# Finer first tiles, a deeper attention pipeline, two plain gate-value pairs and an early down projection in a two-block transformer kernel

## The chip, the cores and the metric

The kernel runs on one core of a Trainium2 chip. The metric is the time of one execution on the device in microseconds (us). Runs of the kernel before took 2423.92, 2426.95 and 2432.35 us; the median is 2426.95 us.

## The reference

Two transformer blocks work on one sequence of 1024 tokens with 1024 features, all in float32. What matters here is the first block and its feed-forward part:

```python
h = rms_norm(x, mix_norm_g)
proj = h @ w_in                       # stick-breaking attention, RWKV, spatial gating, ...
...
up = causal_dwconv(h2 @ w_up, conv_w) # D_FF = 2816: 2816 gate and 2816 value columns
gate, val = jnp.split(up, 2, axis=-1)
x = x1 + (jax.nn.silu(gate) * val) @ w_down
```

The stick-breaking attention (four heads of 64 features) and the spatial gating (a layer norm over 256 features, then a causal 128x128 mix of tokens) are two of four branches between the first projection and the feed-forward part. A second block with other mixers follows.

## The kernel before, in words

**Precision.** Every large matrix product is made of three float32 products. A matrix is split into a rounded part (a cast on ScalarE, ACT; `split`, L99 to L101) and the rest (a subtraction on VectorE, DVE, L101), and hi x hi, hi x lo and lo x hi are added up in PSUM. So each operand of TensorE (PE) costs one cast on ACT and one subtraction on DVE. One matmul instruction has a 128x128 weight tile and 512 moving columns.

**Order of the work.** Python code issues the instructions; a scheduler may move them on their engine unless they are pinned (`keep_in_program_order`) or urgent (`high_priority`). Each engine runs its list in order. `mingle` and `braid` (L130 to L144) interleave two generators: so many steps of the sparse one per step of the dense one.

**Start.** `Norm` (L170) loads the gain row as a 128x1024 broadcast `grow` on ACT's DMA queue. Eight tiles of 128 tokens (`xt`) are normalized (`put`), transposed on PE and split into `hh` and `hl` (`turn`). After four tiles `first_steps` multiplies the first half of the tokens (512) with the first two column tiles of the attention's q and k; the other four tiles are braided into that, and the second half follows. These 96 matmuls of 512 columns are recorded under L123.

**Phase 1.** The projection of the branches (dense, L123) is braided with the stick-breaking attention at the rate `RSB`. Per head and half of the queries, `score` computes the score tiles (L383) and the attention weights (a scan on DVE, L411, then POOL). `pv_steps` (L325) transposes them (L350) into the one PSUM bank `pt`, splits that into `pth` and `ptl`, and multiplies both with the values (L334, L335) one step later (`lag=1`). The spatial gating's norm runs on DVE beside it (L491 to L498).

**Up projection.** 22 units, each with 128 gate and 128 value columns. A unit uses a Strassen-like scheme of seven block products (p1 to p7) of 12 matmuls in place of eight (L1171). It needs sums of the activations' quadrants R2 (the split tiles T1 to T4 and B22), made once at its start (L1277 to L1287; two of these subtractions on GpSimd, POOL), and sums of the weights per unit (POOL). Unit 0 is computed plainly, with eight products, while the T tiles are made. `gate` (L1245) is a 3-tap convolution (ACT, then two steps on DVE), a tanh on ACT and one DVE step (L1249); `value` (L1251) a convolution with weights halved in `vw` and a multiplication on POOL (L1253). The product goes to one DRAM tensor `gg` on the queue of SyncE (SP).

**Down projection.** It loops over two token halves j, two column halves c and the 22 row tiles fi. For each fi it loads a tile of `w_down` (`wr`, L1428) and, for j = 0, one of `gg` (`s`, L1425), splits both, and issues 12 matmuls (L1439 to L1441). The tile pool `slots` for `s` opens after the up projection's pools are closed.

Of the kernel before, what the change touches and what calls it, by code (L numbers as in the profile page):

```python
# [31 lines left out]
RSB, RRW = 0.6, 1.27  # L32
# [33 lines left out]
def kernel(ctx: ExitStack, tc: tile.TileContext, A: dict, out: bass.AP, stop=None):  # L66
# [31 lines left out]
    G.memset(zero1, 0.0)  # L98
    def split(hi, lo, src, eng=None):  # L99
        S.copy(hi, src)  # L100
        (eng or V).tensor_tensor(lo, src, f(hi), op=ALU.subtract)  # L101
# [68 lines left out]
    class Norm:  # L170


        def __init__(self, pool, psum, gain, hi, lo):
            self.pool, self.psum, self.hi, self.lo = pool, psum, hi, lo
            self.g = pool.tile([128, D], F32, name="grow", bufs=1)
            S.dma_start(self.g, gain.partition_broadcast(128))
# [63 lines left out]
    with tc.tile_pool(name="n0", bufs=2) as n0, tc.tile_pool(name="n0p", bufs=2, space=PSUM) as n0p:  # L240
        nm = Norm(n0, n0p, A["mix_norm_g"], hh, hl)
# [10 lines left out]
        def first_steps(j):  # L252
            for c in range(2):
                if j == 0:
                    first.append((mmp.tile([128, T], F32, name="mm"), *sb_qk_weights(c)))
                yield from mm3_steps(*first[c], hh, hl, NK, js=(j,))

        for _ in norm_steps(range(4)):
            pass
        S.dma_start(pv, A["pvec"])  # L260
        S.dma_start(rv, A["rvec"].partition_broadcast(128))
        braid(first_steps(0), norm_steps(range(4, 8)), 0.5)
        for _ in first_steps(1):
            pass
# [128 lines left out]
    def sb_head(h, j, parts):  # L393
# [51 lines left out]
    mx = pj.tile([128, NT, 256], F32, name="mx")  # L445
    wc = pj.tile([128, 4, 128], F32, name="wc")
    S.dma_start(wc, A["sg_wT"].rearrange("g s t -> s g t"))
# [74 lines left out]
    def phase1_steps():  # L522
# [9 lines left out]
        yield from sg_mix()  # L532
        for p in range(2):
            yield from sg_out(p)
# [580 lines left out]
    gg_d = dram.tile([NF * 128, T], F32, name="gg")  # L1115
# [6 lines left out]
    class Unit:  # L1122
# [51 lines left out]
        def bank(self):  # L1174
            return upp.tile([128, 512], F32, name="ac", bufs=4)
# [6 lines left out]

        def plain(self, n):
# [61 lines left out]
        def gate(self):  # L1245
            a = self.conv(self.g, [PV("ffn_conv_w", 2 * NF * i + self.fi) for i in range(3)])
            self.th = up2.tile([128, T], F32, name="th")
            S.activation(self.th, a, AF.Tanh, scale=0.5)
            V.scalar_tensor_tensor(self.th, self.th, 1.0, a, op0=ALU.add, op1=ALU.mult)  # L1249

        def value(self):  # L1251
            b = self.conv(self.v, [vw[:, NF * i + self.fi:NF * i + self.fi + 1] for i in range(3)])
            G.tensor_tensor(b, self.th, b, op=ALU.mult)  # L1253
            (nc.sync if self.fi < NF - 1 else G).dma_start(gg_d[self.fi * 128:(self.fi + 1) * 128, :], b)
# [27 lines left out]
    v.w1()  # L1282
    G.tensor_tensor(R2[1, 0], R2[1, 0], R2[1, 1], op=ALU.subtract)
    v.sums()
    split(*T3, R2[0, 1])
    v.w2()
    split(*T4, R2[1, 0])  # L1287
    str_.close()
    up2 = stu.enter_context(tc.tile_pool(name="up2", bufs=1, reuse_waits="tile"))
    u.copies()  # L1290
    vw = up2.tile([128, 3 * NF], F32, name="vw")
    tc.keep_in_program_order(V.tensor_scalar(vw.rearrange("p (i f) -> p i f", i=3),
                                             PV("ffn_conv_w", 0, 6 * NF).rearrange("p (i e f) -> p i e f", i=3, e=2)[:, :, 1, :],
                                             0.5, None, op0=ALU.mult))
    tables = None
    for n in range(1, NF):
        u, v, w = us[n], us[n + 1] if n < NF - 1 else None, us[n - 1]
        u.p1()
        if n == 1:
            u.w4()  # L1300
        if v:
            v.load()
        if n > 1:
            w.p4()
            w.value()
            u.w3()
# [13 lines left out]
        if n > 1:  # L1320
            u.p2()
            u.c11()
        else:
            u.w3()
# [15 lines left out]
    stw.close()  # L1340
    slots = st3.enter_context(tc.tile_pool(name="slots", bufs=NF, reuse_waits="tile"))
# [70 lines left out]
    with tc.tile_pool(name="dw", bufs=1, side="right", reuse_waits="tile") as dw:  # L1412
# [5 lines left out]
        for j in range(2):  # L1418
            for c in range(2):
                acc = [bank(n) for n in (("ip", "ip", "tp", "tp"), ("lt", "lt", "ho", "iq"),  # L1420
                                         ("ip", "ip", "lt", "lt"), ("ho", "iq", "ip", "ip"))[2 * j + c]]
                for fi in range(NF):
                    if j == 0:
                        g_ = f(slot(c))
                        nc.sync.dma_start(g_, gg_d[fi * 128:(fi + 1) * 128, c * 512:(c + 1) * 512])  # L1425
                        gg.setdefault(fi, {})[c] = g_
                    raw = dw.tile([128, 512], F32, name="wr", bufs=3)
                    nc.sync.dma_start(raw, A["w_down"][fi * 128:(fi + 1) * 128, c * 512:(c + 1) * 512])  # L1428
                    wh, wl, gh, gl = [dw.tile([128, 512], F32R, name=name, bufs=2) for name in ("dwh", "dwl", "gh", "gl")]
                    with tc.high_priority():  # L1430
                        split(wh, wl, raw)
                        split(gh, gl, gg[fi][j])
                    if (j, c, fi) == (0, 0, 1):
                        dn = std.enter_context(tc.tile_pool(name="dn", bufs=1, reuse_waits="tile"))
                    if j and c:
# [8 lines left out]
                if nm is None:  # L1444
                    nm = Norm(dn, ipx, A["norm_gain_2"], hh, hl)
                    fg = dn.tile([128, D], F32, name="fg")
                    S.dma_start(fg, A["final_norm_g"].partition_broadcast(128))
                if c == 0:
                    xs = []
                    for i in range(4):  # L1450
                        x2 = dn.tile([128, D], F32, name="x2", bufs=4)
                        nc.sync.dma_start(x2, x1_d[(4 * j + i) * 128:(4 * j + i + 1) * 128, :])
                        xs.append(x2)
# [554 lines left out]
```

## Time and profile before

| what | before |
|---|---|
| median of the runs | 2426.95 us |
| the profiled execution, its own time | 2424.3 us |
| its span, first to last instruction | 2422.6 us |
| PE busy | 2322.5 us (96%) |
| DVE busy | 1467.4 us (61%) |
| ACT busy | 1067.3 us (44%) |
| POOL busy | 583.3 us (24%) |
| mean granted TensorE clock | 0.989 |

Times in the views are counted from the start of the span. The time that a run reports exceeds the span by 1.7 us. PE is busy for all but 100.1 us of the span, and a stretch counts as busy whether PE runs at its full clock or at the lower level; the granted clock is shown beside it. A matmul's own duration is longer than the distance to the next start, since matmuls are pipelined.

### The profile page before, as it was taken

Reading aid. Unit: us, or ns where it says so; the run is one execution under the profiler, and the core shown is the slowest. Engines: PE = TensorE matmul, PEld = TensorE weight load, DVE = VectorE, ACT = ScalarE, POOL = GpSimd, SP = SyncE. Lnnn points to the kernel's source line nnn. Section 1 sums busy time; section 2 is a strip of 40 time slices with the busy share of each in tenths; the row PEclk is TensorE's granted clock in tenths of the full one; section 3 lists DMA queues with packets and bytes.
Section 4 is the critical chain, followed back from the end, with each engine's and each line's share of the span. In section 5 each row is a group of like instructions: output and inputs, shape, how many; then the busy total and the mean of one; then the engine's idle time right before and its main releaser. Section 6 shows DMA issues by size and latency. Waiting matters only on the chain.

```text
span 2422.6 us, 31192 instructions
## 1 busy us (share of the span) xinstructions
PE 2322.5 (96%) x11330; PEld 1883.0 (78%) x11330; DVE 1467.4 (61%) x2357; ACT 1067.3 (44%) x1973; POOL 583.3 (24%) x582
## 2 busy tenths in 40 slices
PE   6999899999999999998999997999999999999999
PEld 5887676778777887877788886888798777787787
DVE  4245753578455534579888885556756525678842
ACT  4344433222443323444444342446556525669840
POOL 0122310113223111036555552000023100126510
PEclk9999999999999999999999998999999999999999
DMA  4332115454333258412222224734523647766433
GB/s 153 96 100 83 45 60 165 156 170 138 104 95 105 94 163 240 153 36 79 88 87 81 87 79 152 238 101 150 166 87 109 172 140 206 196 174 186 120 115 134
DMA packets 280442, 309.08 MB, mean 128 GB/s; under 512 B 14928, under 2 KB 209120, under 8 KB 280288
## 3 DMA queue, kind: packets, MB, share of 16 engines
q1 hardware_dynamic: 241296, 266.26, 36.2%
q10 hardware_dynamic: 38848, 40.31, 5.2%
q8 instruction: 89, 1.46, 0.3%
q14 instruction: 65, 0.53, 0.1%
q0 software_dynamic: 144, 0.52, 0.1%
HBM read 217.80 MB, written 89.23 MB: 127 GB/s over the span
## 4 chain that ended last, share of the span: by engine, by line
PE 45%; DMA 5%; DVE 4%; ACT 3%; issue 2%; POOL 1%; SPq 0%; POOLq 0%; ACTq 0%; DVEq 0%
PE ac L1171 11%; PE ip L1171 4%; PE ip L1493 3%; PE tp L350 1%; PE ip L1382 1%; PE ip L1383 1%; PE ip L1384 1%; PE iq L334 1%; PE lt L1777 1%; PE iq L335 1%; DMA wr<-in_w_in_dram 1%; PE ip L1441 1%; PE ip L1043 1%; PE ip L1439 1%; PE ip L1440 1%
## 5 line engine op out<-in xcount | busy, mean ns | idle before, releaser
L123 PE MATMUL mm<-hh,whi 128*128 128x512 f32 x896 | 304.6, 411 | 1.6 <-ACT hh L100 0.9
L123 PE MATMUL mm<-hl,whi 128*128 128x512 f32 x896 | 290.1, 395 | 0.0
L123 PE MATMUL mm<-hh,wlo 128*128 128x512 f32 x896 | 288.4, 393 | 1.3 <-DVE wlo L115 1.3
L100 ACT CAST whi<-wraw 128x1024 fp32r<-128x1024 f32 (+1 forms) x117 | 99.8, 853 | 262.7 <-PE mm L123 197.7
L123 PEld LDWEIGHTS mm<-hh,wlo 128*128 128x128 f32 x896 | 168.6, 189 | 38.8 <-DVE wlo L115 1.9
L123 PEld LDWEIGHTS mm<-hl,whi 128*128 128x128 f32 x896 | 168.1, 189 | 36.0 <-DVE hl L101 0.4
L101 DVE TENSOR_TENSOR wlo<-wraw,whi 128x1024 fp32r<-128x1024 f32 (+1 forms) x117 | 118.2, 1013 | 120.4 <-ACT whi L100 114.6
L123 PEld LDWEIGHTS mm<-hh,whi 128*128 128x128 f32 x896 | 158.9, 190 | 37.7 <-issue 7.1
L167 POOL TENSOR_TENSOR rs<-rs,negh 128x1 f32<-128x1 f32 x32 | 19.5, 612 | 381.1 <-DVE rs L166 381.1
L101 DVE TENSOR_TENSOR gl<-s,gh 128x512 fp32r<-128x512 f32 x88 | 60.7, 690 | 80.3 <-ACT gh L100 77.9
L1781 ACT ACTIVATE p<-p,mn 128x640 f32<-128x640 f32 (+7 forms) x128 | 99.5, 778 | 12.4 <-DVE mn L1779 12.1
L926 POOL TENSOR_TENSOR acc<-acc,pacc 128x1024 f32<-128x1024 f32 x20 | 50.7, 2536 | 199.8 <-DVE acc L921 144.6
L100 ACT CAST uhi<-s 128x1024 fp32r<-128x1024 f32 x42 | 44.1, 1053 | 122.9 <-PE ip L1171 87.6
L101 DVE TENSOR_TENSOR ptl<-tp,pth 128x512 fp32r<-128x512 f32 (+3 forms) x144 | 78.0, 555 | 31.8 <-ACT pth L100 30.6
L100 ACT CAST gh<-s 128x512 fp32r<-128x512 f32 x88 | 54.6, 621 | 94.3 <-PE tp L1440 35.6
L101 DVE TENSOR_TENSOR ulo<-s,uhi 128x1024 fp32r<-128x1024 f32 x42 | 88.0, 2097 | 4.9 <-ACT uhi L100 4.9
L100 ACT CAST pth<-tp 128x512 fp32r<-128x512 f32 (+3 forms) x144 | 66.9, 477 | 43.4 <-PE tp L350 41.3
L1253 POOL TENSOR_TENSOR cv<-th,cv 128x1024 f32<-128x1024 f32 x22 | 53.6, 2434 | 128.6 <-issue 90.2
L334 PE MATMUL iq<-pth,v 128*128 128x512 f32 x192 | 71.7, 375 | 7.8 <-DVE t L1806 4.1
L350 PE MATMUL tp<-cv,p 128*128 128x128 f32 x432 | 71.8, 277 | 1.6 <-DVE ptl L101 1.4
L1808 POOL TENSOR_TENSOR zz<-zz,rdb 128x512 f32<-128x512 f32 x16 | 20.6, 1290 | 216.0 <-DMA qh<-aq 128.2
L1493 PE MATMUL ip<-h3h,zh 128*128 128x512 f32 x192 | 65.6, 409 | 3.7 <-DVE zt L1499 3.7
(591 smaller groups left out, 6437.1 us busy)
## 6 DMA issues: line engine op xcount, KB each, us to landing
wraw<-in_w_in_dram SPq DMA_DIRECT2D x60, 512.0 KB, 4.1
wraw<-in_w_up_dram SPq DMA_DIRECT2D x44, 512.0 KB, 3.9
wr<-in_w_down_dram SPq DMA_DIRECT2D x88, 256.0 KB, 2.9
merged<-acc SPq DMA_DIRECT2D x28, 512.0 KB, 2.9
s<-gg SPq DMA_DIRECT2D x44, 256.0 KB, 4.5
gg<-cv SPq DMA_DIRECT2D x21, 512.0 KB, 2.6
pacc<-merged SPq DMA_DIRECT2D x20, 512.0 KB, 4.1
x<-x ACTq DMA_DIRECT2D x16, 512.0 KB, 2.7
```

Source lines behind the costliest of these rows:

```text
L100: S.copy(hi, src)
L101: (eng or V).tensor_tensor(lo, src, f(hi), op=ALU.subtract)
L123: PE.matmul(ps[:, c0 + j * 512:c0 + (j + 1) * 512], w[:, k, :], x[j][:, k, :], start=(k == 0 and w is wh and x is xh), stop=(k == nkt - 1 ...
L334: PE.matmul(po[-1][:, w], vh[:, k, :], ph_[:, w], start=(k == 0), stop=False)
L335: PE.matmul(po[-1][:, w], vh[:, k, :], pl_[:, w], start=False, stop=(k == nk - 1))
L350: PE.transpose(pt[:, i * 128:(i + 1) * 128], P[p0 + i][:, k * 128:(k + 1) * 128], ident)
L926: G.tensor_tensor(ac, ac, pa, op=ALU.add)
L1043: PE.matmul(po, ml[:, k, :], W[c][k][0], start=False, stop=(k == NK - 1))
L1171: PE.matmul(acc, a[:, k, :], b[:, k, :], start=(start and k + n == 0), stop=(k == 3 and n == 2), skip_group_check=True)
L1253: G.tensor_tensor(b, self.th, b, op=ALU.mult)
L1493: PE.matmul(ps[j], w[:, k, :], x[j][:, n, :], start=(n == 0 and w is wh and x is hh), stop=(n == 7 and bool(last)))
L1781: S.activation(pr_[:, :L], pr_[:, :L], AF.Exp, scale=-1.0, bias=mn[:, c:c + 1], accum_out=self.den[:, i:i + 1])
```

## The change

1. **Start.** The gain row is loaded once (4 KB on SP's queue) and spread over the partitions by two matmuls with a single contraction row into PSUM (`spread`). The first two column tiles are done by quarters of the tokens: 192 matmuls with 256 columns. They begin after two token tiles and are braided with the others at 0.25. SP's list begins with the row, two `xt`, the two weight tiles, four `xt`, two weight tiles, two `xt`, then `pv` and `rv`, which were on ACT's queue before the second weight load.
2. **Phase 1.** `RSB` goes from 0.6 to 0.7. `pv_steps` gets a lag of two steps and three buffers for `pth` and `ptl`; the bank `pt` stays single. `mx` shares the tile `vt`, and the mixing steps are mingled into the first output step.
3. **Up projection.** Units 0 and 1 are both plain. Unit 1's split weights (`own`) lie in the memory of T3, its accumulators in the banks `tp` and `ip`. The two subtractions of 128x2048 on POOL go to DVE, the gate is one Silu activation on ACT, the multiplication in `value` goes from POOL to DVE, and `vw` is gone. `gg` is 22 DRAM tensors; the last two are written on POOL's queue.
4. **Down projection.** The rows fi = 0 and 1 of the first pass are loaded and split inside the last unit (`down0`). From fi = 2 the loads of `s` and `wr` alternate on SP. The loads of `grow`, `fg` and four `x2` come at fi = 11 of the c = 0 passes.

```diff
-RSB, RRW = 0.6, 1.27
+RSB, RRW = 0.7, 1.27
...
+            self.g = psum.tile([128, D], F32, name="g", bufs=1)
+            for q in range(2):
+                PE.matmul(self.g[:, q * 512:(q + 1) * 512], ones, row[:, q * 512:(q + 1) * 512], start=True, stop=True)
...
+            for ps, wh, wl in first:
+                for k in range(NK):
+                    for w, x, last in ((wh, hh, 0), (wh, hl, 0), (wl, hh, 1)):
+                        PE.matmul(ps[:, q * 256:(q + 1) * 256], w[:, k, :], x[q // 2][:, k, s],
...
-        for _ in norm_steps(range(4)):
+        for _ in norm_steps(range(2)):
             pass
...
+        for q in range(3):
+            braid(first_steps(q), norm_steps(range(2 * q + 2, 2 * q + 4)), 0.25)
...
-            t1 = f(sb.tile([128, 512], F32R, name="ptl", bufs=2))[0:64]
+            t1 = f(sb.tile([128, 512], F32R, name="ptl", bufs=3))[0:64]
...
-        return [lambda i=i: score(i) for i in range(4 * j, 4 * j + 4)], pv_steps(sb, sb_po, sb_pt, v2[:, :, h, :], P, [(j, 0, evict)], 2)
+        return [lambda i=i: score(i) for i in range(4 * j, 4 * j + 4)], pv_steps(sb, sb_po, sb_pt, v2[:, :, h, :], P, [(j, 0, evict)], 3, 2)
...
-            S.activation(self.th, a, AF.Tanh, scale=0.5)
-            V.scalar_tensor_tensor(self.th, self.th, 1.0, a, op0=ALU.add, op1=ALU.mult)
+            S.activation(self.th, a, AF.Silu)
...
-            G.tensor_tensor(b, self.th, b, op=ALU.mult)
+            V.tensor_tensor(b, self.th, b, op=ALU.mult)
...
+    v.own(*[x.rearrange("p a c -> p (a c)").rearrange("p (w k c) -> p w k c", w=2, k=NK) for x in T3])
+    v.plain(0)
+    v.plain(1)
     split(*B12, R2[0, 1])
     split(*B22, R2[1, 1])
-    u.plain(2)
-    u.plain(3)
+    for x in (u, v):
+        x.plain(2)
+        x.plain(3)
...
-    G.tensor_tensor(R2[0, 1], R2[1, 1], R2[0, 1], op=ALU.subtract)
+    V.tensor_tensor(R2[0, 1], R2[1, 1], R2[0, 1], op=ALU.subtract)
...
+            for fi in range(2):
+                raw = wpool.tile([128, 2, 512], F32, name="wraw")
+                nc.sync.dma_start(raw[:, 0], A["w_down"][fi * 128:(fi + 1) * 128, 0:512])
+                nc.sync.dma_start(raw[:, 1], gg_d[fi][:, 0:512])
...
+                    if c == 0 and fi == NF // 2:
...
+                            pin(nc.sync.dma_start)(x2, x1_d[(4 * j + i) * 128:(4 * j + i + 1) * 128, :])
```

**PE in phase 1**, near the end of one head's second half. `mm` is the projection; `pth` and `ptl` are the two parts of a transposed tile of weights, `pt` is the bank, `sg` the weights. The brackets name the engine whose work the instruction waits for. Before:

```order
L123 MATMUL mm<-hh_77,wlo 128x512
L334 MATMUL po<-pth,v_551 128x384 [waits Activation_49]
L335 MATMUL po<-ptl,v_551 128x384 [waits DVE_49]
L350 MATMUL pt<-cv,sg_922 128x128 [waits PE_49]
L350 MATMUL pt<-cv,sg_979 128x128
L123 MATMUL mm<-hh_76,whi 128x512
```

Now:

```order
L127 MATMUL mm<-hh_77,wlo 128x512
L357 MATMUL po<-pth,v_652 128x384 [waits Activation_49]
L358 MATMUL po<-ptl,v_652 128x384
L373 MATMUL pt<-cv,sg_1053 128x128 [waits DVE_49]
L127 MATMUL mm<-hh_76,whi 128x512
```

The wait for DVE has moved from the product with `ptl` to the next transpose, one row further on. In both lists it is for the tile that was transposed in the step before; the product with `ptl` now belongs to the step before that.

**DVE at the start of the up projection**, from the first subtraction on the quadrants `r` (R2). `t1l` to `t4l` and `b2l` are the low parts of the split activations, `wlo`, `a2l` and `ulo` those of weights. Before:

```order
L1277 TENSOR_TENSOR r_7411<-r_7412,r_7411 128x2048
L101 TENSOR_TENSOR t4l<-r_7412,t4h 128x2048
L101 TENSOR_TENSOR b2l<-r_7414,b2h 128x2048
L101 TENSOR_TENSOR t1l<-r_7411,t1h 128x2048
L1280 TENSOR_TENSOR r_7414<-r_7414,r_7411 128x2048
L101 TENSOR_TENSOR t3l<-r_7412,t3h 128x2048
L101 TENSOR_TENSOR t2l<-r_7414,t2h 128x2048
L101 TENSOR_TENSOR wlo<-wraw,whi 128x1024
L101 TENSOR_TENSOR t4l<-r_7413,t4h 128x2048
```

Now:

```order
L1313 TENSOR_TENSOR r_7511<-r_7512,r_7511 128x2048
L105 TENSOR_TENSOR t3l<-wraw,t3h 128x1024 x2
L105 TENSOR_TENSOR t4l<-r_7512,t4h 128x2048
L105 TENSOR_TENSOR b2l<-r_7514,b2h 128x2048
L105 TENSOR_TENSOR t1l<-r_7511,t1h 128x2048
L1315 TENSOR_TENSOR r_7512<-r_7514,r_7512 128x2048
L105 TENSOR_TENSOR ulo<-s_8548,uhi 128x1024
L1316 TENSOR_TENSOR r_7514<-r_7514,r_7511 128x2048
L1323 TENSOR_TENSOR r_7513<-r_7513,r_7514 128x2048
L105 TENSOR_TENSOR t2l<-r_7514,t2h 128x2048
L105 TENSOR_TENSOR wlo<-wraw,whi 128x1024 x2
L1328 TENSOR_TENSOR t3l<-r_7512,t3h 128x2048
```

Two splits of unit 1's weights (`t3l<-wraw`) and the two subtractions from POOL (L1315, L1323) have come in; the real T3 is split after all the rest.

**SP's queue around the start of the down projection.** `gg<-cv` are the last units' results, `wr` the rows of `w_down`, `s` those of `gg`; `x<-x` are the loads of `x2`. Before:

```order
L1254 DMA gg<-cv 128x1024 x3
L1428 DMA wr<-in_w_down_dram 128x512 x3
L1452 DMA x_11850<-x_7404 128x1024
L1452 DMA x_11852<-x_7404 128x1024
L1428 DMA wr<-in_w_down_dram 128x512
L1452 DMA x_11854<-x_7404 128x1024
L1428 DMA wr<-in_w_down_dram 128x512
L1452 DMA x_11856<-x_7404 128x1024
L1425 DMA s_11315<-gg 128x512
```

Now:

```order
L1285 DMA gg_8272<-cv 128x1024
L1363 DMA wraw<-in_w_down_dram 128x512
L1364 DMA wraw<-gg_8254 128x512
L1363 DMA wraw<-in_w_down_dram 128x512
L1364 DMA wraw<-gg_8255 128x512
L1285 DMA gg_8273<-cv 128x1024
L1473 DMA s_11439<-gg_8256 128x512
L1479 DMA wr<-in_w_down_dram 128x512
L1473 DMA s_11463<-gg_8257 128x512
```

The four `x2` loads have left this place, and the first rows of `gg` are loaded ahead of the write of unit 19's result.

## Rows read from the trace of the kernel before

**Rows 1.** The page, section 1: busy time, share of the span, instructions.

```profile
PE 2322.5 (96%) x11330; PEld 1883.0 (78%) x11330; DVE 1467.4 (61%) x2357; ACT 1067.3 (44%) x1973; POOL 583.3 (24%) x582
```

**Rows 2.** Waits of PE: waiter <- releaser: us in total, times, longest.

```profile
PE ip L1439 <- ACT gh L100: 13.8, 1, 13.8
PE tp L193 <- DVE xn L184: 13.0, 4, 9.4
PE po L335 <- DVE ptl L101: 11.4, 6, 6.3
```

**Rows 3.** Windows: length, busy (count) of PE, PEld, DVE, ACT, POOL; clock, DMA share, GB/s.

```profile
0.00:57.20 57.20, 36.21 (x161) 27.91 (x162) 26.50 (x48) 24.00 (x54) 5.63 (x18) 1.00 0.47 147
```

**Rows 4.** Timeline of the start: start, duration, instruction, [idle before <-releaser].

```profile
8.58 1.42 DVE L184 SCALAR_TENSOR_TENSOR xn<-xt,rs,grow 128x512 f32<-128x512 f32 x2 [1.88 <-DMA grow<-in_mix_norm_g_dram]
...
25.68 0.79 PE L123 MATMUL mm<-hh,whi 128*128 128x512 f32 x1 [0.68 <-ACT hh L100]
...
44.63 1.04 PE L193 MATMUL tp<-cv,xn 128*128 128x128 f32 x8
...
54.68 0.39 PE L123 MATMUL mm<-hl,whi 128*128 128x512 f32 x1
...
57.18 0.61 PE L123 MATMUL mm<-hh,whi 128*128 128x512 f32 x2
```

**Rows 5.** Timeline of PE late in the second block, around two matmuls of 256 columns.

```profile
2339.44 0.28 PE L334 MATMUL iq<-pth,v 128*128 128x256 f32 x1
2339.55 0.28 PE L335 MATMUL iq<-ptl,v 128*128 128x256 f32 x1
2339.68 0.40 PE L1877 MATMUL lt<-foh,mh 128*128 128x512 f32 x1
```

**Rows 6.** The page, section 5: weight loads of L123 (busy, mean ns | idle).

```profile
L123 PEld LDWEIGHTS mm<-hh,wlo 128*128 128x128 f32 x896 | 168.6, 189 | 38.8 <-DVE wlo L115 1.9
```

**Rows 7.** Timeline of phase 1: PE's longest wait and DVE before it.

```profile
278.88 2.28 DVE L411 TENSOR_TENSOR_SCAN ex<-kp,zero 128x1024 f32<-128x1024 f32 x1
281.08 0.40 DVE L101 TENSOR_TENSOR ptl<-pt,pth 128x256 fp32r<-128x256 f32 x1
...
281.53 0.58 PE L335 MATMUL po<-ptl,v 128*128 128x256 f32 x1 [6.26 <-DVE ptl L101]
```

**Rows 8.** Timeline of the up projection's start: DVE, POOL and PE.

```profile
1058.89 2.29 DVE L101 TENSOR_TENSOR b2l<-r,b2h 128x2048 fp32r<-128x2048 f32 x1
1059.06 6.58 POOL L1278 TENSOR_TENSOR r<-r,r 128x2048 f32<-128x2048 f32 x1 [8.47 <-DVE t4l L101]
1061.10 6.69 DVE L101 TENSOR_TENSOR t1l<-r,t1h 128x2048 fp32r<-128x2048 f32 x1
...
1079.04 0.80 PE L1171 MATMUL ac<-b0h,whi 128*128 128x512 f32 x1 [5.82 <-ACT cg L1195]
```

**Rows 9.** Windows: the up projection's start, then its steady loop.

```profile
1060.00:1140.00 80.00, 67.71 (x277) 53.68 (x276) 76.21 (x58) 36.13 (x42) 42.48 (x17) 0.94 0.23 67
...
1160.00:1480.00 320.00, 320.00 (x1400) 261.44 (x1399) 267.87 (x237) 130.69 (x148) 164.56 (x80) 1.00 0.24 77
```

**Rows 10.** Groups of instructions from 1160 to 1480 us: busy, mean ns of one.

```profile
L1253 POOL TENSOR_TENSOR cv<-th,cv 128x1024 f32<-128x1024 f32 x16 | 38.8, 2423 | 80.8 <-issue 80.8
...
L1249 DVE SCALAR_TENSOR_TENSOR th<-th,cv 128x1024 f32<-128x1024 f32 x17 | 20.8, 1225 | 9.1 <-ACT th L1248 9.1
```

**Rows 11.** Timeline where the down projection starts.

```profile
1492.12 0.40 PE L1171 MATMUL ac<-t4h,a2l 128*128 128x512 f32 x1
...
1498.42 1.27 DVE L1242 SCALAR_TENSOR_TENSOR cv<-cx,vw,cv 128x1022 f32<-128x1022 f32 x1
...
1499.38 9.38 SPq L1425 DMA_DIRECT2D s<-gg  x12
...
1506.34 0.79 PE L1439 MATMUL ip<-dwh,gh 128*128 128x512 f32 x1 [13.82 <-ACT gh L100]
```

**Rows 12.** Windows: the first matmuls of the down projection.

```profile
1506.00:1510.00 4.00, 3.66 (x9) 2.84 (x10) 1.36 (x2) 0.91 (x2) 0.00 (x0) 0.50 1.01 351
```

More of the change, by code (lines that the diff above doesn't have):

```diff
@@ L250, in norm_steps, with first_steps @@
                 yield
[L252 to L256, printed above, removed]
-        for _ in norm_steps(range(4)):
-            pass
[L260 to L263, printed above, removed]
+        def first_steps(q):
+            s = slice(q % 2 * 256, q % 2 * 256 + 256)
+            for ps, wh, wl in first:
+                for k in range(NK):
+                    for w, x, last in ((wh, hh, 0), (wh, hl, 0), (wl, hh, 1)):
+                        PE.matmul(ps[:, q * 256:(q + 1) * 256], w[:, k, :], x[q // 2][:, k, s],
+                                  start=(k == 0 and w is wh and x is hh), stop=(k == NK - 1 and bool(last)))
+                    yield
+        for _ in norm_steps(range(2)):
+            pass
+        first += [(mmp.tile([128, T], F32, name="mm"), *sb_qk_weights(c)) for c in range(2)]
+        for q in range(3):
+            braid(first_steps(q), norm_steps(range(2 * q + 2, 2 * q + 4)), 0.25)
+        tc.keep_in_program_order(nc.sync.dma_start(pv, A["pvec"]))
+        tc.keep_in_program_order(nc.sync.dma_start(rv, A["rvec"].partition_broadcast(128)))
+        for _ in first_steps(3):
             pass
@@ L531, in phase1_steps @@
             yield
-        yield from sg_mix()
-        for p in range(2):
-            yield from sg_out(p)
+        mix = sg_mix()
+        for n, _ in enumerate(sg_out(0)):
+            if n % 2 == 0:
+                next(mix, None)
+            yield
+        yield from sg_out(1)
         yield from short_conv(1)
@@ L1109, in block2_tables @@
         yield
-    gg_d = dram.tile([NF * 128, T], F32, name="gg")
+    gg_d = [dram.tile([128, T], F32, name=f"gg{fi}") for fi in range(NF)]
     stu = ExitStack()
@@ L1174, in bank @@
         def bank(self):
+            if self.fi == 1:
+                return ipx.tile([128, 512], F32, name="tp" if len(self.b) < 2 else "ip", bufs=2)
             return upp.tile([128, 512], F32, name="ac", bufs=4)
@@ L1181, in wv, with own @@
             (self.a21, self.a22) = zip(halves4(hi), halves4(lo))
+        def own(self, hi, lo):
+            for i in range(2):
+                split(hi[:, i], lo[:, i], self.raw[i])
+            (self.a11, self.a12), (self.a21, self.a22) = [zip(halves4(hi[:, i]), halves4(lo[:, i])) for i in range(2)]
         def plain(self, n):
@@ L1339 @@
     st2.close()
-    stw.close()
-    slots = st3.enter_context(tc.tile_pool(name="slots", bufs=NF, reuse_waits="tile"))
+    slots = None
     def slot(j, ncol=512):
@@ L1430 @@
[L1430 to L1433, printed above, removed]
-                        dn = std.enter_context(tc.tile_pool(name="dn", bufs=1, reuse_waits="tile"))
+                    early = j + c == 0 and fi < 2
+                    if (j, c, fi) == (0, 0, 2):
+                        stw.close()
+                        slots = st3.enter_context(tc.tile_pool(name="slots", bufs=NF, reuse_waits="tile"))
@@ new lines @@
+                    late = {10: [0], 12: [1]}.get(fi, []) if c == 0 else []
+                    for x in ([] if early else [fi]) + late if j == 0 else []:
+                        g_ = f(slot(c))
+                        tc.keep_in_program_order(nc.sync.dma_start(g_, gg_d[x][:, c * 512:(c + 1) * 512]))
+                        gg.setdefault(x, {})[c] = g_
+                    if early:
+                        wh, wl, gh, gl = down0[fi]
+                    else:
+                        raw = dw.tile([128, 512], F32, name="wr", bufs=3)
+                        ld = nc.sync.dma_start(raw, A["w_down"][fi * 128:(fi + 1) * 128, c * 512:(c + 1) * 512])
+                        if j == 0:
+                            tc.keep_in_program_order(ld)
+                        wh, wl, gh, gl = [dw.tile([128, 512], F32R, name=name, bufs=2) for name in ("dwh", "dwl", "gh", "gl")]
+                        with tc.high_priority():
+                            split(wh, wl, raw)
+                            split(gh, gl, gg[fi][j])
@@ L1443 @@
                         spread.pop(0)()
[L1444 to L1453, printed above, removed]
                 for i in range(4):
```

96 lines of the change are left out of this document (55 added, 41 removed).

## The prediction

> **What bounds the kernel now.** The first view is the page's list of busy times: PE works 2322.5 of the 2422.6 us of the span [rows 1]. So only about 100 us are idle, and a change that leaves the matmuls as they are can win no more than a part of these, and what runs at the lower clock behind them. PE's waits say where they lie [rows 2]: one of 13.8 us ahead of the down projection's first matmul, 13.0 us for the normalized rows of the start, 11.4 us in six waits for `ptl` in phase 1. The other engines' busy shares tell nothing here; each place is then read in its own stretch. In the first 57.2 us PE is busy for 36.2, so 21.0 are idle [rows 3]. From 1060 to 1140 us, the up projection's start, it is busy for 67.7 of 80 with a granted clock of 0.94, while DVE is busy for 76.2 [rows 9]; there DVE is the bound. From 1160 to 1480 us PE is busy for all 320 us and DVE for 267.9: there PE is the bound, and nothing that DVE or POOL save is worth anything.
>
> **The change part by part.** Prices are of the profiled execution: 2422.6 us of span and 1.7 around it, 2424.3. The runs' median is 2.7 above that. A measurement of this kernel tells about 0.3%, 7.3 us, from no change.
>
> *Start.* Now DVE's first row multiplication starts at 8.58 after 1.88 us of waiting for the broadcast gain, the first projection matmul at 25.68, and the first matmul of the next pair of columns at 57.18 [rows 4]. Four tiles thus take 25.68 - 8.58 = 17.1 us, 4.3 each. With the gain row loaded by 4 KB, the first tile can start about 1.9 us earlier, at 6.7, and after two tiles, at 15.3, the products can begin; I take 16, as the first weight tile's cast comes between. Two limits follow. By PE: 192 matmuls of 256 columns at 0.115 (starts of 2339.44, 2339.55 and 2339.68 [rows 5]) are 22.1 us, six remaining tiles' transposes at 1.04 for eight [rows 4] are 6.2, so 44.3. By the tiles: 6.7 + 8 x 4.3 = 41.1, then 48 matmuls, 5.5 us: 46.6. The later one holds. The work itself costs nothing more: 96 matmuls at 0.227 (11 starts from 54.68 to 57.18 [rows 4]) were 21.8. **Gain 57.2 - 46.6 = 10.6**, between 6 (the two weight splits, 2 x 1.2 us on DVE and about as much on ACT, stretch the tiles' pace) and 13 (PE sets the end). The two spreading matmuls, the memset and the moved loads of `pv` and `rv` lie beside the tiles' loads; their cover is that nobody reads them before the first set ends.
>
> *Phase 1.* The longest wait, 6.26 us, ends when DVE has done a scan of 2.28 and then a `ptl` of 0.40 [rows 7]. DVE has worked off its list in order and came late, so the data was ready and DVE was not. The change gives PE no more room here than it seems: with one bank `pt`, the next transposes cannot start before `ptl` of the tile in the bank is made, so the wait moves by one row, from the product to the transpose. What remains is a different mixing: more attention steps per projection step, and the norm of the spatial gating meets other work. I cannot follow that through. **I take 3 of the 11.4** [rows 2], with the bounds +11 (all waits gone) and -6 (one more like the longest).
>
> *Up projection, start.* From 1060 to 1140 PE loses 12.3 us idle, and at a granted clock of 0.94 another 0.06 x 80 = 4.8 us [rows 9]: 17.1. A step of 128x2048 takes DVE 2.29 us, but 6.69 while a subtraction of 6.58 runs on POOL beside it [rows 8]. Two subtractions run on POOL there, so by this pair DVE loses some 2 x 4.4 us. With both on DVE its chain up to the second T tile is eight steps of 2.29 and three of 1.2, 22.0 us, without such a pair. Over it lie sixteen plain products, 16 x 12 x 0.227 = 43.6 us of PE, so no step of this chain is waited for. What is late next is T3: its memory holds unit 1's weights until the last plain product, so T3's and T4's splits, two convolutions, the first value multiplication and unit 2's second pair of weights (2 x 2.29, 7 x 1.2 and three of 0.7, some 15 us with the first cast of T3 ahead, 2 us) stand on DVE between the last plain product and the product p7. PE has five products ahead of p7 that need none of this (one of them the next unit's first), 60 matmuls or 13.6 us, so it waits about 2 us there. Unit 1 costs 12 matmuls more, 2.7 us. **Gain 17.1 - 2.7 - 2 = 12.4**; at best 14.4, at worst 3 (POOL's sums of weights run beside and stretch DVE's steps as above, and p7 is late by 10 more).
>
> *Up projection, steady loop.* A DVE step of 1.225 goes (L1249) and a multiplication of the same 128x1024 comes, which I price the same; POOL loses 2.42 [rows 10]. A unit has 84 matmuls, 19.05 us, so 320 us are 16.8 units and DVE's slack is (320 - 267.9) / 16.8 = 3.1 us a unit [rows 9]. Net cost 0, covered by that slack; if it were used up, each further microsecond would count twenty times. Silu for tanh is one ACT step for one.
>
> *Down projection, start.* Up's last matmul starts at 1492.12; SP issues the loads of `s` from 1499.38 only, and the next matmul starts at 1506.34 after 13.82 us [rows 11]. Then nine matmuls fill 3.9 us at a granted clock of 0.50 [rows 12] instead of 2.0, about 1.8 us lost. With rows 0 and 1 split beforehand, 24 matmuls (5.4 us) follow at once. Row 2's loads no longer stand behind the `x2` loads, so data is not late; its splits on DVE are, behind the last unit's convolutions: these end 7.2 us after PE's last matmul now (1498.42 + 1.27 against 1492.5) [rows 11], and the step that goes and the one that comes are alike. So PE waits about 1.7 us. The loads that have moved to fi = 11 (`grow`, `fg`, four `x2`, each 0.5 MB, at 351 GB/s [rows 12] 8.5 us) are covered by three buffers of `wr`, 5.4 to 8.2 us of matmuls: 0 to 3 us, I take 1. **Gain 15.6 - 1.7 - 1 = 12.9**, between 9 and 15.6.
>
> **Sum:** 10.6 + 3 + 12.4 + 12.9 = 38.9, so 2424.3 - 38.9 = **2385 us**. All lower ends together would be a gain of 12 (2412), all upper ends one of 54 (2370).
>
> **The rivals.** *1. The waits only move.* DVE does as many steps at the up start as before, and in phase 1 the mixing is no better: the up start gives 3 and phase 1 nothing. For it: DVE is busy for 76.2 of 80 us there [rows 9], and the bank `pt` is single. Against it: the steps of 6.7 go, and the cover of plain products doubles. Gain 10.6 + 0 + 3 + 12.9 = 26.5: 2398. *2. Weight loads bound the narrow matmuls.* Every 256 columns now need a weight load, whose own record is 0.189 us [rows 6], more than 0.115. If these don't overlap, the quarters take 192 x 0.189 = 36.3 us in place of 22.1, PE's limit is 58.5 and the start loses 1.3: 2397. Against it: weight loads are as many as matmuls [rows 1], and yet starts lie 0.11 and 0.13 apart [rows 5], and eight transposes of 128 columns fit into 1.04 [rows 4], though only in short groups. The Trainium skill (TensorE: Matmul & The Clock Gate, sections "Back-to-back issue gap" and "LDWEIGHTS (loading the stationary operand)") says that in a stream of weight loads and matmuls both set the spacing, and that a load of 128 columns takes about 107 ns; with loads and 256-column matmuls one after the other the quarters would last about 43 us by an estimate from that page, side by side 22; the pair in the trace speaks for side by side, and no run here shows a long stream. *3. Everything fits.* The phase 1 waits and the up start's go as well: 2372. *4. DVE becomes the bound of the loop (slower).* The value multiplication waits for Silu in DVE's list, and the sums and splits that PE needs queue behind it. Price: what DVE loses above 3.1 us a unit, 20 times. It decides from 5.0 us a unit, where the 38.9 are used up; at 6 it gives 20 x 2.9 = 58 us, 2443. For it: L1249 already waited 9.1 us in 17 units, 0.5 each [rows 10]. Against it: that is a tenth of what is needed, and POOL's 2.42 us a unit no longer slow DVE's steps. That the change does not do what it says is phase 1's case, in rival 1.
>
> **How the numbers follow.** The forecast has a chance of 0.58, rival 1 0.20, rival 2 0.08, rival 3 0.09, rival 4 0.03; 0.02 is left for several small losses that end within 7.3 us of no change. The first four are faster, but the low ends of rival 1 with a phase 1 that loses 6 come near the bound: faster 0.92, same 0.05, slower 0.03. The range is from rival 3 less 4 us (the runs lie that far apart) to rival 1 and 2 with a phase 1 that loses 6 and the median's 2.7: 2368 to 2407.
>
> **What would show it.** Start: first projection matmul at about 16 us, PE's starts there 0.115 apart, the first full-width matmul at about 47. Phase 1: waits for `ptl` under the transposes' line, 8 us or less in sum. Up start: no wait of PE over 3 us, no DVE step over 4 us, one stall of about 2 us before unit 2's p7, the granted clock near 1.00. Loop: PE busy throughout, 19.05 us a unit. Down start: no gap over 3 us. Wrong would be: a start after 55 us (rival 2), a PE wait of 5 us at the up start (rival 1), or idle slices of PE in the loop (rival 4).

## The result and the profile after

In four runs beside four of the kernel before, the changed kernel took 2395.61 us (2394.49 to 2402.20) against 2429.65 (2423.92 to 2432.47): a ratio of 0.9872, 95% interval 0.9857 to 0.9886. On another occasion, in five runs, it was 2396.76 against 2423.25, ratio 0.9891 (0.9875 to 0.9906). So it is faster by 1.1 to 1.3%, 26 to 34 us. The forecast was 2385, its range 2368 to 2407. The profiled execution spans 2393.6 us against 2422.6.

The page's busy times of the changed kernel answer to [rows 1]:

```profile
PE 2319.7 (97%) x11442; PEld 1888.7 (79%) x11442; DVE 1421.0 (59%) x2349; ACT 1065.4 (45%) x1970; POOL 515.7 (22%) x556
```

PE's idle time fell from 100.1 to 73.9 us. Where the 29.0 us of the span come from is read from six places that both programs pass: the first matmul over all tokens behind the first set, the first one of the RWKV branch (`tp<-xwa,wa`, about the end of phase 1), the first and last of the up projection, and the first one behind the down projection. Lengths of the stretches between them in us, each from one trace; the third and the last stretch run code that the change does not touch:

| kernel | start | phase 1 | to the up projection | up | down | second block | span |
|---|---|---|---|---|---|---|---|
| before | 57.2 | 333.4 | 657.1 | 444.4 | 263.9 | 666.6 | 2422.6 |
| changed | 49.5 | 333.1 | 654.7 | 437.3 | 258.2 | 660.8 | 2393.6 |
| changed, again | 49.8 | 332.6 | 660.1 | 437.3 | 256.6 | 659.9 | 2396.3 |

The four changed stretches gave 7.7, 0.3, 7.1 and 5.7 us, 20.8 together. The other 8.2 lie in untouched code. Over the fourteen traces on which this document rests the third stretch lies between 653.5 and 660.1 us and the last between 659.1 and 666.6 (the longest is the one of the kernel before), so part of the 8.2 is what executions differ by. How much of the 26 to 34 us of the runs is owed to such code, these traces don't settle.

A single trace also tells a stretch only so far. Where the code of the stretch is that of the changed kernel, the start takes 48.5 to 50.9 us in eleven traces, phase 1 331.9 to 335.1 in ten, the up projection 437.3 to 440.1 and the down projection 254.9 to 259.0 in seven each. A difference of less than some 3 us between two traces, 4 in the down projection, shows nothing by itself; there the waits must speak.

**Start.** The timeline of the changed kernel answers to [rows 4]; columns as there:

```profile
2.78 3.75 PE L185 MATMUL g<-row,ones 1*128 1x512 f32 x4 [2.78 <-DMA row<-in_mix_norm_g_dram]
7.54 1.40 DVE L201 SCALAR_TENSOR_TENSOR xn<-xt,rs,g 128x512 f32<-128x512 f32 x2 [0.76 <-POOL rs L171]
8.34 1.97 PE L210 MATMUL tp<-cv,xn 128*128 128x128 f32 x8 [1.81 <-DVE xn L201]
...
16.49 0.56 PE L275 MATMUL mm<-hh,whi 128*128 128x256 f32 x1
...
18.47 0.41 PE L275 MATMUL mm<-hl,whi 128*128 128x256 f32 x1
18.69 0.41 PE L275 MATMUL mm<-hh,wlo 128*128 128x256 f32 x1
...
19.37 0.28 PE L275 MATMUL mm<-hh,whi 128*128 128x256 f32 x1
19.49 0.28 PE L275 MATMUL mm<-hl,whi 128*128 128x256 f32 x1
...
36.99 1.41 DVE L201 SCALAR_TENSOR_TENSOR xn<-xt,rs,g 128x512 f32<-128x512 f32 x2 [0.73 <-POOL rs L171]
...
41.78 0.28 PE L275 MATMUL mm<-hh,wlo 128*128 128x256 f32 x1
41.90 1.03 PE L210 MATMUL tp<-cv,xn 128*128 128x128 f32 x8
...
49.52 0.63 PE L127 MATMUL mm<-hh,whi 128*128 128x512 f32 x2
```

The gain row no longer holds up the first tile; POOL's `rs` does, and only 1.0 us was won there (8.58 to 7.54). The narrow matmuls are 0.12 us apart, the first ten of them about 0.21. The last tile is normalized at 38.4 us, but its transposes start at 41.90, directly behind a matmul: they stand behind the third quarter in PE's list. From the first matmul to the set's end PE is nearly full (window, then its waits for the projection's operands):

```profile
16.50:49.50 33.00, 30.89 (x240) 29.50 (x239) 20.29 (x37) 14.85 (x35) 2.88 (x7) 1.00 0.24 77
```

```profile
PE mm L275 <- DVE hl L105: 1.4, 3, 0.6
PE mm L275 <- ACT hh L104: 0.7, 3, 0.2
```

**Phase 1.** PE's waits in the changed kernel from 49.5 to 382.6 us, to set beside the one line of 11.4 us in six waits of [rows 2]:

```profile
PE pt L373 <- DVE ptl L105: 6.8, 7, 2.2
PE pt L540 <- DVE stg L541: 3.0, 2, 1.9
PE tp L621 <- ACT xwa L598: 1.9, 1, 1.9
PE pt L508 <- DVE stg L465: 1.4, 1, 1.4
PE pt L540 <- DVE ptl L105: 1.1, 1, 1.1
```

The long wait is gone, but smaller ones have come, some for other steps on DVE. The stretch as one window, first before, then changed (length, busy of PE, PEld, DVE, ACT, POOL, clock, DMA):

```profile
57.20:390.60 333.40, 320.11 (x1498) 257.69 (x1496) 169.89 (x211) 126.92 (x186) 71.47 (x134) 0.98 0.28 82
```

```profile
49.50:382.60 333.10, 317.91 (x1500) 255.96 (x1498) 172.44 (x213) 128.41 (x188) 71.47 (x135) 1.00 0.30 89
```

PE is idle for 15.2 us now where it was for 13.3, and busy for 2.2 us less, at a granted clock of 1.00 where it was 0.98; the two cancel. In the second trace of the changed kernel the clock of this stretch is 0.99.

**Up projection.** The changed kernel's longest wait there and what lies behind it: DVE's `a2l` is the last reader of a buffer (`wraw`) into which unit 3's weights are loaded, POOL's first sum waits for that load, and PE for the split of the sums (`uhi`):

```profile
1093.47 0.68 DVE L105 TENSOR_TENSOR a2l<-wraw,a2h 128x512 fp32r<-128x512 f32 x1
...
1098.33 1.57 POOL L1170 TENSOR_TENSOR s<-wraw 128x512 f32<-128x512 f32 x1 [36.09 <-DMA wraw<-in_w_up_dram]
...
1104.94 0.79 PE L1197 MATMUL ac<-t2h,uhi 128*128 128x512 f32 x1 [2.49 <-ACT uhi L104]
```

Its two windows that lose most, and the loop [rows 9]:

```profile
1100.00:1120.00 20.00, 17.37 (x63) 13.30 (x62) 17.54 (x16) 9.73 (x12) 13.85 (x7) 0.83 0.27 80
1120.00:1140.00 20.00, 18.49 (x82) 15.00 (x81) 19.13 (x20) 8.74 (x10) 7.25 (x4) 1.00 0.44 130
...
1160.00:1480.00 320.00, 320.00 (x1409) 263.51 (x1408) 242.45 (x235) 131.55 (x151) 121.87 (x61) 1.00 0.27 84
```

DVE's two gaps of some 5 us before 1083 are covered by the plain products. From there it is nearly always busy until 1140, and PE waits for it. In the loop PE is full as before, and DVE is busy for 25 us less of 320.

**Down projection.** The changed kernel, to set beside [rows 11]:

```profile
1482.57 0.50 PE L1503 MATMUL ip<-dwl,gh 128*128 128x512 f32 x1 [1.92 <-DVE dwl L105]
...
1500.97 2.01 SPq L101 DMA_DIRECT2D x<-x  x4
...
1513.18 0.62 ACT L104 CAST gh<-s 128x512 fp32r<-128x512 f32 x1 [6.22 <-DMA s<-gg]
...
1515.20 1.22 PE L1502 MATMUL ip<-dwh,gh 128*128 128x512 f32 x2 [3.75 <-ACT dwh L104]
```

And its windows around the second gap:

```profile
1508.00:1512.00 4.00, 3.45 (x16) 2.52 (x14) 0.00 (x0) 0.00 (x0) 0.00 (x0) 1.00 1.03 412
...
1516.00:1520.00 4.00, 4.00 (x10) 3.09 (x10) 1.24 (x2) 0.51 (x1) 0.00 (x0) 0.50 0.76 250
```

The gap of 13.82 us is down to 1.92. A new one of 3.75 comes at fi = 12. Ahead of it the DMA engines are full (1.03, 412 GB/s) with the six loads of fi = 11, four of which are issued at 1500.97, and ACT gets its tile of `gg` 6.22 us late; behind it the matmuls run at half the clock.

### The profile page after: what moved, and what is told of

Same layout as the page of the kernel before. It is cut to its first block, busy times and chain, and to the rows that moved or that the text cites. A ratio compares the mean times of both kernels' runs of the same rounds, so it can differ in the third digit from the quotient of the medians.

```text
span 2393.6 us, 31342 instructions
## 1 busy us (share of the span) xinstructions
PE 2319.7 (97%) x11442; PEld 1888.7 (79%) x11442; DVE 1421.0 (59%) x2349; ACT 1065.4 (45%) x1970; POOL 515.7 (22%) x556
## 5 line engine op out<-in xcount | busy, mean ns | idle before, releaser
L127 PE MATMUL mm<-hh,whi 128*128 128x512 f32 x864 | 289.8, 409 | 1.6 <-ACT th L937 1.6
L127 PE MATMUL mm<-hl,whi 128*128 128x512 f32 x864 | 275.7, 393 | 0.0
L127 PE MATMUL mm<-hh,wlo 128*128 128x512 f32 x864 | 273.9, 391 | 0.0
L127 PEld LDWEIGHTS mm<-hh,wlo 128*128 128x128 f32 x864 | 162.0, 188 | 35.2
L127 PEld LDWEIGHTS mm<-hl,whi 128*128 128x128 f32 x864 | 161.6, 188 | 34.6
L127 PEld LDWEIGHTS mm<-hh,whi 128*128 128x128 f32 x864 | 151.7, 189 | 33.7 <-issue 6.9
L1834 ACT ACTIVATE p<-p,mn 128x640 f32<-128x640 f32 (+7 forms) x128 | 99.4, 778 | 12.5 <-DVE mn L1832 12.2
L1170 POOL TENSOR_TENSOR s<-wraw 128x512 f32<-128x512 f32 x20 | 41.7, 2083 | 185.9 <-DVE ulo L105 117.0
L358 PE MATMUL iq<-ptl,v 128*128 128x512 f32 x192 | 68.8, 364 | 0.0
```

The lines of the kernel that those rows point to most:

```text
L127: PE.matmul(ps[:, c0 + j * 512:c0 + (j + 1) * 512], w[:, k, :], x[j][:, k, :], start=(k == 0 and w is wh and x is xh), stop=(k == nkt - 1 ...
L358: PE.matmul(po[-1][:, w], vh[:, k, :], pl_[:, w], start=False, stop=(k == nk - 1))
L1170: G.tensor_tensor(x[:, 1], a21, a22, op=ALU.add)
L1834: S.activation(pr_[:, :L], pr_[:, :L], AF.Exp, scale=-1.0, bias=mn[:, c:c + 1], accum_out=self.den[:, i:i + 1])
```

## The experiments

Most kernels undo one part of the changed kernel; the table gives their stretches in us.

| kernel | start | phase 1 | to the up projection | up | down | second block | span |
|---|---|---|---|---|---|---|---|
| x_start | 57.7 | 333.1 | 656.8 | 437.4 | 254.9 | 665.9 | 2405.8 |
| x_phase | 50.0 | 333.5 | 653.5 | 439.2 | 258.2 | 662.4 | 2396.8 |
| x_lag | 49.1 | 338.2 | 653.9 | 440.1 | 257.7 | 664.4 | 2403.4 |
| x_gate | 48.5 | 331.9 | 656.5 | 447.3 | 255.3 | 660.1 | 2399.6 |
| x_mulpool | 50.9 | 334.3 | 655.7 | 443.1 | 259.7 | 659.1 | 2402.8 |
| x_bgate | 57.4 | 333.6 | 656.8 | 441.1 | 265.5 | 661.1 | 2415.5 |
| x_pool | 48.7 | 333.0 | 655.0 | 437.4 | 257.8 | 660.9 | 2392.8 |
| x_w4 | 49.3 | 333.6 | 654.8 | 437.6 | 259.0 | 659.5 | 2393.8 |
| x_noearly | 50.1 | 332.5 | 656.7 | 437.5 | 261.0 | 659.3 | 2397.1 |
| x_spread | 49.8 | 335.1 | 653.8 | 438.8 | 248.9 | 661.0 | 2387.4 |
| x_spread5 | 48.7 | 332.2 | 659.5 | 440.0 | 251.4 | 660.9 | 2392.7 |

### x_start: the old start in the changed kernel

```diff
-        nm = Norm(n0, n0p, A["mix_norm_g"], hh, hl, spread=n0p)
+        nm = Norm(n0, n0p, A["mix_norm_g"], hh, hl)
...
-        for _ in norm_steps(range(2)):
+        for _ in norm_steps(range(4)):
```

> The changed kernel with the old start alone (broadcast gain on ACT's queue, halves of 512 columns after four tiles). Theory: the start's 7.7 us (57.2 against 49.5 at the first set's end) are its own, so the set ends at about 57 us and the rest is moved by 7 to 8 us, with the same gaps behind it: 2402 us. Rival: the early end only moves a wait to phase 1, whose loads now meet the first set; then phase 1 wins back a part and the whole loses 3 us or less.

The set ends at 57.7 us, 8.2 later, and phase 1 is as long as in the changed kernel: the start's gain is its own. The time was 2407.8 us; of the 12.2 us of span, 8.2 are the start's, and the rest is in stretches with the same code.

### x_phase and x_lag: the old phase 1, and the old lag alone

```diff
-RSB, RRW = 0.7, 1.27
+RSB, RRW = 0.6, 1.27
...
-pv_steps(sb, sb_po, sb_pt, v2[:, :, h, :], P, [(j, 0, evict)], 3, 2)
+pv_steps(sb, sb_po, sb_pt, v2[:, :, h, :], P, [(j, 0, evict)], 2)
...
```

x_phase has both and the old order of the mixing; x_lag has the second alone (a lag of one step with two buffers).

> The changed kernel with the old phase 1 (rate 0.6, lag of one step, mixing ahead of the first output). Theory: the waits on ptl come back under the products' line, with one of over 4 us behind the spatial gating's norm on DVE, and the stretch from the end of the first set to the first matmul of the output projection is 2 to 4 us longer. Rival: the long wait of the kernel before was an accident of its phase against the start; then no wait is over 3 us and the stretch is as long as now, within 1 us.

> The changed kernel with a lag of one step and two buffers again, rate 0.7 and the mingled mixing kept. Theory: with one bank for the transposes the lag gives no room, so this stretch is as long as in the changed kernel within 1 us, and the waits on ptl stand at the products instead of the transposes. Rival: the longer lag is what hides DVE's lateness; then 3 us or more come back here.

In x_phase the waits for `ptl` are back, 11.4 us in six as in [rows 2], the longest behind the scan as in [rows 7]. Its timeline:

```profile
270.35 2.29 DVE L434 TENSOR_TENSOR_SCAN ex<-kp,zero 128x1024 f32<-128x1024 f32 x1
272.55 0.40 DVE L105 TENSOR_TENSOR ptl<-pt,pth 128x256 fp32r<-128x256 f32 x1
...
273.01 0.58 PE L358 MATMUL po<-ptl,v 128*128 128x256 f32 x1 [6.30 <-DVE ptl L105]
```

But the stretch is 333.5 us against 333.1 and 332.6: half of each theory held. The wait is no accident of the start, it belongs to the old phase 1; and taking it away won nothing, since other waits of the same sum came. x_lag is 5.1 us longer (338.2, 3.1 above the longest of the ten traces with the new phase 1), with the wait at the products again. Its timeline:

```profile
276.87 0.79 PE L358 MATMUL po<-ptl,v 128*128 128x512 f32 x1 [3.61 <-DVE ptl L105]
```

So at the rate 0.7 the longer lag does seem to give room, against the theory and the prediction, as far as one trace can show it. x_lag and x_phase both have the old lag and differ by the rate and the order of the mixing: these two cost 4.7 us (338.2 against 333.5), about what the lag gives back. Which of the two costs it was not tried.

### x_gate, x_mulpool and x_bgate: the gate

x_gate is the changed kernel with the old gate, x_mulpool the one with Silu but the multiplication on POOL, x_bgate the kernel before with the new gate.

```diff
-            S.activation(self.th, a, AF.Silu)
+            S.activation(self.th, a, AF.Tanh, scale=0.5)
+            V.scalar_tensor_tensor(self.th, self.th, 1.0, a, op0=ALU.add, op1=ALU.mult)
...
-            V.tensor_tensor(b, self.th, b, op=ALU.mult)
+            G.tensor_tensor(b, self.th, b, op=ALU.mult)
...
```

> The changed kernel with the old gate: tanh, a step on DVE, halved value weights, the multiplication on POOL. Theory: PE is the bound of the loop, so a unit stays at 19.05 us and the loop is as long within 0.5 us; at the up start POOL's multiplications stretch DVE's steps and PE loses 1 to 4 us more; at its end the last unit's chain is 1 us longer. Rival: DVE has become the bound in the changed kernel or is near it; then units get shorter or longer here by 0.3 us or more.

> The changed kernel with Silu, and only the value multiplication back on POOL. The full old gate made the up projection 10 us longer (447.3 against 437.3 us). Theory: POOL's steps beside DVE stretch DVE's where DVE is the bound, so the multiplication's place is most of it: 443 to 448 us. Rival: the wait of DVE's extra step for the tanh holds its list: then 437 to 440 us here.

> The kernel before with the new gate alone (Silu, multiplication on DVE). Theory: DVE is the bound of the up start there too, so the gate alone shortens the up projection from 444.4 us by 4 to 10, and the second plain pair with the moved subtractions is worth only the rest of the 7.1 us that the whole change won there. Rival: with the sums of the quadrants on DVE's path ahead of everything, the gate is worth under 2 us in the old order and the plain pair is what uncovers its gain.

The old gate makes the up projection 10.0 us longer (447.3), far more than expected, and none of it in the later loop: from 1180 to 1480 us PE is busy throughout. PE's waits from 1037 to 1180 us in x_gate:

```profile
PE ac L1197 <- DVE u L1249: 6.3, 2, 4.7
PE ac L1197 <- ACT uhi L104: 4.2, 1, 4.2
PE ac L1197 <- DVE ulo L105: 1.4, 2, 0.8
```

The multiplication's place alone is 5.8 of the 10.0 (443.1), as the theory had it. In the old order the same gate wins only 3.3 us (441.1), less than expected and little more than what traces of one code differ by. The long wait for the copies, 5.8 us as in [rows 8], stays, and the other waits hardly shrink. PE's waits from 1047 to 1150 us in x_bgate:

```profile
PE ac L1171 <- ACT cg L1195: 5.8, 1, 5.8
PE ac L1171 <- DVE cx L1228: 3.9, 1, 3.9
PE ac L1171 <- DVE u L1217: 1.1, 1, 1.1
```

And the plain pair, with the subtractions on DVE and the old gate, is 447.3 - 444.4 = 2.9 us slower than before, so it wins nothing. Neither is worth what both are together, 7.1. How much of the multiplication's 5.8 us is DVE's steps stretched beside POOL, and how much POOL's own list (weight sums queued behind multiplications), these runs do not separate.

### x_pool: the two subtractions back on POOL

```diff
-    V.tensor_tensor(R2[0, 1], R2[1, 1], R2[0, 1], op=ALU.subtract)
+    G.tensor_tensor(R2[0, 1], R2[1, 1], R2[0, 1], op=ALU.subtract)
```

> The changed kernel with the two subtractions of 128x2048 back on POOL. Theory: two DVE steps grow from 2.3 to 6 or 7 us, but 43.6 us of plain products lie over the chain, so PE waits at most 1 us more. Rival: the subtractions on DVE are what took the up start's waits away; then PE loses 5 us or more there.

DVE's step beside POOL is as long as in [rows 8], and it costs nothing: 437.4 us. The two steps in x_pool's timeline:

```profile
1050.28 6.53 POOL L1315 TENSOR_TENSOR r<-r,r 128x2048 f32<-128x2048 f32 x1 [10.64 <-DVE t4l L105]
...
1052.27 6.69 DVE L105 TENSOR_TENSOR t1l<-r,t1h 128x2048 fp32r<-128x2048 f32 x1
```

DVE's step ends 2.15 us after POOL's (1058.96 and 1056.81), and so it does in [rows 8] (1067.79 and 1065.64). A step of 2.29 us thus seems to stand until POOL's is done, rather than both running at a slower pace.

### x_w4: unit 2's second split earlier

```diff
     tables = None
+    us[2].w4()
     u.gate()
```

> The changed kernel, unit 2's second split of the value weights made ahead of the plain units' convolutions. Theory: that split holds the buffer into which unit 3's value weights are loaded, so the load starts about 5 us earlier, POOL's sums too, and the wait of 2.5 us for unit 3's first pair (with some 3 us lost at the lower clock behind it) goes; gain 3 to 5 us. Rival: POOL's own sums or the ACT order hold that pair; then the wait stays, within 1 us.

The load did come earlier, and POOL's first sum starts at 1093.94 in place of 1098.33. The wait for unit 3's pair is gone, but PE now waits 1.90 us for unit 2's, and for DVE's `cx`, `u` and `ulo` behind it; the stretch is 437.6. Its waits from 1037 to 1150 us:

```profile
PE ac L1197 <- DVE cx L1260: 2.5, 2, 1.6
PE ac L1197 <- ACT uhi L104: 1.9, 1, 1.9
PE ac L1197 <- DVE ulo L105: 0.5, 1, 0.5
```

Neither theory held as put: the named buffer was the cause of the named wait, and the time is the same. The waits that are left are mostly for DVE, which is busy for 39.1 of the 40 us from 1100 to 1140 (36.7 in the changed kernel), so its list as a whole seems to be what is late.

### x_noearly: no early rows

```diff
-                    early = j + c == 0 and fi < 2
+                    early = False
...
```

> The changed kernel without the two early rows: rows 0 and 1 of the down projection are loaded and split like the others, the x2 loads stay at fi = 11. Theory: the early rows cover the last unit's convolutions on DVE, so PE now stands idle for about 7 us after its last matmul of the up projection and runs some 4 us at the lower clock, in place of 1.9 and 3: 5 to 7 us longer there. Rival: it is the order of the loads that took the 13.8 us away and the splits are made in time; then the gap is 3 us or less.

The timeline of x_noearly where the down projection starts:

```profile
1481.80 0.79 PE L1492 MATMUL ip<-dwh,gh 128*128 128x512 f32 x1 [4.59 <-ACT dwh L104]
...
1484.79 0.79 PE L1493 MATMUL ip<-dwl,gh 128*128 128x512 f32 x1 [2.20 <-DVE dwl L105]
```

The gap is 6.8 us in two parts, as the theory had it, 4.9 more than 1.92. The stretch is only 2.8 to 4.4 us longer than in the two traces of the changed kernel (258.2 and 256.6), in part because the second gap shrank (2.86 after 3.75), and only 2.0 above the longest of the seven traces of that code; the gap itself is the evidence. So of the first gap of 13.8 us the early rows took 4.9 and the rest of the change 7.0. The moved loads are the likely cause of these 7.0; no run undoes them alone.

### x_spread, x_spread5 and x_after5: the six loads apart

```diff
-                    if c == 0 and fi == NF // 2:
+                    if c == 0 and fi in (5, 7, 9, 13, 15, 17):
...
```

One of `grow`, `fg` and the four `x2` at each of these rows. x_spread5 is the same kernel run five times, x_after5 the changed kernel beside it.

> The changed kernel with the gain, final gain and four x2 loads at fi = 5, 7, 9, 13, 15 and 17 in place of all at 11. Theory: the 3 MB at once held back the rows behind them on SP's queue; spread out they fit between, so the wait of 3.8 us and the lower clock behind it go: gain 5 to 7 us in the first pass. Rival: the traffic as such is too much for this pass, and small waits of the same sum appear at each of the six places; gain under 2 us.

> The changed kernel with the six loads spread over rows 5 to 17. Theory: 6 us or more under the changed kernel, 0.983 to 0.986 of the kernel before, with the down projection at 249 us in place of 258. Rival: the 9 us seen in one run are partly chance; then the ratio is 0.986 or more.

> The changed kernel again, for the spread of its stages: the second block, which the change does not touch, within 2 or 3 us of the run before; ratio 0.986 to 0.989.

The second gap is gone, with PE full where it stood; x_spread's window:

```profile
1510.00:1520.00 10.00, 10.00 (x46) 8.29 (x45) 5.18 (x8) 4.44 (x8) 0.00 (x0) 1.00 0.83 285
```

The down projection takes 248.9 and 251.4 us against 258.2 and 256.6, 7.2 less on the mean. In five runs each on one occasion the median is 2391.45 us against 2396.76 of the changed kernel, 5.3 less; the ratios to the kernel before are 0.9866 (0.9848 to 0.9885) and 0.9891 (0.9875 to 0.9906). The intervals overlap, so the time alone does not settle it. The gap does: it stands in all ten traces of kernels with the six loads at fi = 11 (2.9 to 4.8 us) and in neither of the two with the loads apart. x_spread5 just missed its 6 us and its ratio of 0.983 to 0.986, so by the ratio the rival holds, and part of the first run's gain was chance; its median is still the lowest here. x_after5's second block is 0.9 us from that of the first trace, as expected, and its ratio lies at the edge of the 0.986 to 0.989.

## Why the prediction was right or wrong

**The time lies in the range, but all four terms were too large.** 2395.6 us is 10.6 above the number. Rival 4 did not come: PE is full in the loop. The four stretches gave 20.8 us in the trace where 38.9 were forecast. By them alone the time would be 2424.3 - 20.8 = 2403.5 us, near the range's upper end; that it came nearer to the number is owed to 8.2 us in untouched code, which is luck.

**Start, forecast 10.6, measured 7.7.** The first matmul came at 16.49 (forecast 16), the narrow ones 0.12 apart (0.115), so rival 2 is out: 192 x 0.12 are 23.0 us. Of the two estimates from the Trainium skill (TensorE: Matmul & The Clock Gate, "Back-to-back issue gap" and "LDWEIGHTS (loading the stationary operand)"), the trace agrees with the one for loads and matmuls side by side. What failed is the choice between the two limits. The prediction let the tiles set the set's end (46.6) and had PE done at 44.3. In the trace PE set it: the last tile was ready 3.5 us before PE took up its transposes. From 16.5 us on PE's work was put at 28.3 us and took 33.0. Of the 4.7 more, 0.9 come from 0.12 in place of 0.115, some 1 from the first ten matmuls at about 0.21, and 2.1 from waits at the start of each later quarter for the splits of its tokens, which the sum left out. The gain row was also misread: its wait of 1.88 us was taken as all won, but in the kernel before `rs` was done at 7.43 only, so that 1.15 could be won:

```profile
6.85 0.58 POOL L167 TENSOR_TENSOR rs<-rs,negh 128x1 f32<-128x1 f32 x1 [5.83 <-DVE rs L166]
```

**Phase 1, forecast 3, measured 0.3.** The bounds held; the reason was half right, and 0.3 is within what traces differ by. The wait did move to the transposes, and the new mixing did exchange waits. Not borne out is "gives PE no more room here than it seems": without the longer lag x_lag is 5.1 us longer. What the prediction did not have is that the higher rate and the new order of the mixing together cost about as much.

**Up start, forecast 12.4, measured 7.1.** The cover of plain products worked as put: no wait until p7, where the sum of 0.31 and 0.64 us stood against the 2 forecast. (The steps that the prediction lists are 15.1 us; with the cast of 2 ahead of them and 13.6 of cover they would give 3.5 rather than 2.) Mis-sized was what is late next. The prediction followed DVE up to p7 and stopped; the waits of 2.49 and 1.51 us come in the next unit, unit 3, with the clock at 0.83 from 1100 to 1120 us, 3.4 us lost. All of these add up to 8.4 against 2. It also gave the gain to the wrong steps: the two subtractions are worth nothing (x_pool), and the gate, priced at 0 "covered by that slack", is worth 10.0 there (x_gate). The slack of 3.1 us a unit was read from the loop; at the up start DVE has none.

**Down start, forecast 12.9, measured 5.7.** The first gap was 1.92 us (forecast 1.7). The step that failed is "0 to 3 us, I take 1" for the six loads: 3.75 and 4.42 us in the two traces, and behind it matmuls at the lower clock, which the sum left out here although it had counted them for the kernel before. x_spread gives 7.2 of it back.

**The rivals.** Rival 1 (2398) is nearer in time than the forecast, and its phase 1 came true, but not its up start (3, measured 7.1) nor its start and down start. That too is luck.

## What to carry to other kernels

An operation that is free where TensorE is the bound can be worth ten microseconds where another engine is: price it in each stretch apart, and follow the list of the late engine one unit beyond the first wait. Two parts of a change may be worth 3 us or less apart and 7 together (the gate and the plain pair), so undo each from the whole and add each to the old. Where two limits of a stretch lie close, as the tiles' and PE's at the start, put the waits into both before choosing one. Bulk loads that nobody waits for belong between the small ones, not at one place in a queue that others need.

## What the runs showed of the hardware

The two matmuls with one contraction row (two of 512 columns, recorded as four) took 3.75 us; nothing waited for them here. They ran in the first microseconds, where other matmuls too took about twice as long as later (eight transposes 1.97 us, 1.03 at 41.90), so what they cost at the full clock is not shown.

A subtraction of 128x2048 on DVE (2.29 us alone) that meets one on POOL ends 2.15 us after POOL's. This holds for all four such pairs, two in the kernel before and two in x_pool, whether the step then takes 6.69, 6.60 or 5.18 us.

The same stall of 1.92 or 1.93 us at row fi = 2 of the down projection stands in nine traces. In six of them the lower clock followed (0.83 on the mean of the ten us behind it, 1.7 us lost), in x_after5, x_start and x_spread it did not (1.00). So the wait's length alone does not tell whether the clock falls, and a sum with such waits has an uncertainty of 1 to 2 us for each.
